# Weight requests on ACT's DMA queue, with four kinds of instructions raised in priority

## Chip, core and metric

The kernel runs on one core of one Trainium2 chip. The metric is device time in microseconds (us) of that core, median over the runs of a measurement; the profile is one further execution of the same program.

## The reference, cut to what matters

One layer of a decoder with two groups of heads is computed for 512 prompt tokens and for 32 new tokens (8 sequences of 4) behind a paged cache of 2048 positions each. All is float32.

```
h = rmsnorm(x, norm_w)                      # x: 544 tokens x 2048
p = h @ w_in                                # w_in: 2048 x 8192
qa, ka, va, za, qb, fb, ib, zb = split(p, 1024 columns each)
o_a = stick_breaking(qa, ka, va)            # 8 heads of 128; new tokens also see the cache
o_b, s = hgrn2(silu(qb), fb, ib, s0)        # 8 heads, gated linear recurrence
m = concat(head_rmsnorm(o_a) * silu(za), head_rmsnorm(o_b) * silu(zb))
y = final_rmsnorm(x + m @ w_out)            # w_out: 2048 x 2048
```

Stick-breaking attention takes A[t,s] = beta[t,s] times the product of (1 - beta[t,j]) over s < j < t with beta = sigmoid(q.k/sqrt(128) + bias), which the kernel computes with exp, ln and a running sum along the keys. Outputs are y, the new keys and values, and the new recurrent states.

## The kernel before, in words

**Stages.** The tokens are loaded, transposed and split into a rounded part and a rest, `h_hi` and `h_lo` (L338 to L356). Then 64 columns of 128 outputs of the input projection follow one another (`group_a`, L927, and `group_b`, L1007, both through `project`, L381), and then the output projection in 8 column groups (L1124 and L1209). Between the matmuls of the projections the TensorE order holds all other work: prompt attention (`attend`, L455), the recurrence (`hgrn`, L705), and attention of the new tokens over the cache (`decode`, L645), which runs from the first heads of group A to about 0.87 of the projections.

**Weights.** Both projections read their weights in 160 pieces of 512 KB (128 of `w_in`, 32 of `w_out`), in the order of `plan` (L239). Each piece goes through three steps. `load_ahead` (L244) requests it from HBM into a `wraw` tile, of which there are three. `split_ahead` (L252) has ACT cast it into `whi` (L259) and DVE subtract that into `wlo` (L260), of which there are two each. `project` multiplies `whi` with `h_hi` and `h_lo`, and `wlo` with `h_hi` (L401). A piece is requested three ahead of the one in use and split one ahead (`weights_piece`, L268). A `wraw` tile is free again when both halves of its split are done; in the output projection also when TensorE has used it for the sample rows (L1115). A `whi` or `wlo` tile is free when TensorE has done its matmuls. When a column is done, DVE takes it out of PSUM with a multiplication (L408).

**Cache.** Pages of keys are requested in units of 1 MB, four DMAs each (`k_fetch`, L534), into three `kpage` tiles; DVE transposes each unit in place (`k_turn`, L550), and TensorE reads it in `dzp` (L678). Pages of values are requested in blocks of 256 KB (`v_fetch`, L556) into ten `vpage` tiles. One step of `decode` uses two key units and eight value blocks.

**Order.** L164 fixes the order of TensorE and of SyncE (SP) to that of the program text, in which `Flow` (L76) places side work between matmuls by estimated costs and delays. SP issues nearly all loads: weights, key pages, value pages, states and queries. It stands at each request until that request's tile is free, and what is behind it waits. The order on ACT, DVE and POOL is made by the scheduler when the kernel is built: of what it reckons ready at a time, it takes the instruction with the lowest number, which counts along the program text. Each engine then runs its list in that order and stands at an instruction that waits. ACT's own DMA queue holds a few small constants at the start (L298 to L307), the rows of x and `fnw` for the end of the kernel (L1161 to L1166), and half of the output rows (L1189, L1207).

Of the kernel before, what the change touches and what calls it, by code (L numbers as in the profile page):

```python
# [9 lines left out]
F32 = mybir.dt.float32  # L10
# [3 lines left out]
ALU = mybir.AluOpType  # L14
# [126 lines left out]
def hybrid_step(ctx: ExitStack, tc: tile.TileContext, x_prompt, x_sample, cache_k, cache_v, state_s, page_table,  # L141
                norm_w, w_in, gain_a, gain_b, sb_bias, lb_logits, w_out, final_norm_w, consts, masks,
                y_prompt, y_sample, k_prompt, v_prompt, s_prompt, k_sample, v_sample, s_sample):
    nc = tc.nc
# [33 lines left out]
    def mm(n):  # L178
        return 4.0 * max(n, 128) / 2.4


    cst = per.tile([P, C_SELH], F32, name="cst")
    ident = cst[:, C_ID:C_ID + P]
# [14 lines left out]
    rbc = per.tile([P, T], F32, name="rbc")  # L198
# [22 lines left out]
    def in_view(kh, col):  # L221
        return w_in_v[:, 8 * kh:8 * kh + 8, col:col + P]

    def out_view(kq, cg):
        return w_out_v[:, 4 * kq:4 * kq + 4, cg * CG:cg * CG + CG]
# [15 lines left out]
    raws = []  # L241
    taken = [0]

    def load_ahead(n):  # L244
        while len(raws) < min(n, len(plan)):
            kind, k, c = plan[len(raws)]
            view = in_view(k, c) if kind == "in" else out_view(k, c)
            raw = wpool.tile([P, 1024], F32, name="wraw", bufs=3)
            nc.sync.dma_start(raw.rearrange("p (k e) -> p k e", k=view.shape[1]), view)
            raws.append(raw)  # L250

    def split_ahead(n):  # L252
        while len(splits) < min(n, len(plan)):
            i = len(splits)
            load_ahead(i + 1)
            pool, kw = (keep[0], {"bufs": 4}) if i >= len(plan) - 4 else (wpool, {})
            hi = pool.tile([P, 1024], F32R, name="whi", **kw)
            lo = pool.tile([P, 1024], F32R, name="wlo", **kw)
            turns.append(nc.scalar.copy(hi, raws[i]))  # L259
            nc.vector.tensor_tensor(lo, raws[i], hi.bitcast(F32), ALU.subtract)  # L260
            k = 8 if plan[i][0] == "in" else 4
            splits.append([t.rearrange("p (k e) -> p k e", k=k) for t in (raws[i], hi, lo)])

    splits = []
    turns = []
    keep = [None]

    def weights_piece(want):  # L268
        i = taken[0]
        assert plan[i] == want  # L270
        taken[0] += 1
        split_ahead(i + 2)
        load_ahead(i + 4)
        return splits[i]
# [11 lines left out]
    for i in range(NB + 1):  # L286
        n = P if i < NB else NS
        xt = xpool.tile([P, D], F32, name=f"xt{i}", bufs=1)
        cuts = (0, D // 4, D // 2, D) if i == 0 else (0, D // 2, D)
        for a, b in zip(cuts, cuts[1:]):  # L290
            nc.sync.dma_start(xt[:n, a:b], xp[i * P:(i + 1) * P, a:b] if i < NB else xs[:, a:b])
            if i == 0 and a == 0:
                nc.sync.dma_start(ident, consts[:, C_ID:C_ID + P])
                nc.sync.dma_start(nw_rows, norm_w[0].rearrange("(h d) -> h d", d=P))
        xts.append(xt)
        if i == 1:
            load_ahead(2)
# [83 lines left out]
    def project(out, col, first=False):  # L381
        ps = [ps_acc.tile([P, 512], F32, name="pacc", tag="acc") for _ in range(2)]
        pieces = [None, None]
        order = [(kh, half, part) for kh in range(2) for part in range(2) for half in range(2)]
        if first:
            order = [(kh, half, part) for half in range(2) for kh in range(2) for part in range(2)]
        for kh, half, part in order:
            if pieces[kh] is None:
                pieces[kh] = weights_piece(("in", kh, col))
            _, hi, lo = pieces[kh]  # L390
            ts = HALVES[half]
            n = ts.stop - ts.start
            if part == 0:
                todo = [(j, hi, x) for j in range(8) for x in (h_hi[kh], h_lo[kh])]
            else:
                todo = [(j, lo, h_hi[kh]) for j in range(8)]
            for s in range(0, len(todo), STEP):
                yield STEP * (n / 2.4 + 2.0)
                for r in range(s, s + STEP):
                    j, a, x = todo[r]  # L400
                    nc.tensor.matmul(ps[half][:, :n], a[:, j, :], x[:, j, ts],  # L401
                                     start=(kh == 0 and part == 0 and r == 0), stop=(kh == 1 and part == 1 and r == 7))
            if kh == 1 and part == 1 and (half or not first):
                if callable(out):
                    out = out()
                for e in range(2) if first else (half,):
                    ts = HALVES[e]
                    nc.vector.tensor_tensor(out[:, ts], ps[e][:, :ts.stop - ts.start], rbc[:, ts], ALU.mult)  # L408


    def gate(hh, zt, sg):
# [122 lines left out]
    def k_fetch(n):  # L534
        while len(kpending) < min(n, len(kunits)):
            t = dp.tile([P, 4, 512], F32, name="kpage", bufs=3)
            b, gp, h2 = kunits[len(kpending)]
            for i in (0, 2, 1, 3):
                src = kpages[page_value(k_held, b, gp, i), :, h2 * 512:h2 * 512 + 512]
                nc.sync.dma_start(t[32 * i:32 * i + 32], src.rearrange("o (s r) e -> (o r) s e", r=32))  # L540
            kpending.append(t)
# [3 lines left out]
    def k_turn(n):  # L545
        while len(turned) < min(n, len(kunits)):
            k_fetch(len(turned) + 1)
            t = kpending[len(turned)]
            flat = t.rearrange("p s e -> p (s e)")
            nc.vector.transpose(flat, flat)  # L550
            turned.append(t.rearrange("p s (g d) -> p g s d", g=4))

    vunits = [(b, gp, hf, i) for b in range(DB) for gp in range(4) for hf in range(2) for i in range(4)]
# [91 lines left out]
    def decode(start, stop):  # L645
# [4 lines left out]
        for step in range(NSTEP):  # L650
# [10 lines left out]
            if keys:  # L661
                k_turn(2 * step + 1)
                yield 0.0, (0.0 if step == 0 else 14000.0), 0.0, 0.0
                k_turn(2 * step + 2)
# [262 lines left out]
    def group_a():  # L927
        nonlocal ap, dp, tp_, later, earlier
        for h in range(H):
            if h == H - 1:  # L930
                k_fetch(3)
            if h == 2:
                for c in (slice(0, 6 * P), slice(6 * P, NM * P)):
                    lvlf = ap.tile([P, 6 * P], F32, name="lt", tag="lvlf", bufs=1)[:, :c.stop - c.start]
                    nc.gpsimd.dma_start(lvlf, masks[:, c])
                    nc.gpsimd.tensor_copy(lvls[:, c], lvlf)
            qts = []

            def qtile():
                qts.append(atile("qt"))  # L940
                return qts[0]

            for i, c in enumerate(project(qtile, h * P, h == 0)):
                if h == 0 and i == 23:
                    flow.wait(lambda: not flow.side)
                    xstack.close()
                    dp = dstack.enter_context(tc.tile_pool(name="dpool", bufs=1))
                    dcon = dp.tile([P, C_TOT - C_LATER], F32, name="dcon")
                    nc.sync.dma_start(dcon, consts[:, C_LATER:])
                    later, earlier = dcon[:, :P], dcon[:, P:]  # L950
                    tp_ = dstack.enter_context(tc.tile_pool(name="tpool", bufs=1))
                    lvls = tp_.tile([P, NM * P], U8, name="lvls")
                    lvl.extend(lvls[:, P * i:P * i + P] for i in range(NM))
                    ap = astack.enter_context(tc.tile_pool(name="apool", bufs=1))
                yield c
            nc.gpsimd.tensor_copy(q_new[:, h, :], qts[0][:, SEQ:])
            nc.gpsimd.dma_start(q_dram[h], qts[0][:, :SEQ])
        flow.add(decode(H / 64, STOP), 2)
        for h in range(H):
            qt = ap.tile([P, SEQ], F32, name="ql", bufs=2)  # L960
            nc.sync.dma_start(qt, q_dram[h])
            kt = atile("kt")
            yield from project(kt, W + h * P)
            vt = atile("vt")
            yield from project(vt, 2 * W + h * P)
            res = {}
            flow.wait(lambda: not a_side or a_side[-1] not in flow.side)
            a_side.append(flow.add(attend(h, qt, kt, vt, res), 0))
            zt = atile("zt")
            yield from project(zt, 3 * W + h * P)  # L970
            sg = ap.tile([P, T], F32, name="sg")
            gate(h, zt, sg)
            res["zt"] = zt
            if "ot" in res:
                a_side.append(flow.add(finish_head(ap, h, res["ot"], zt, 4500.0), 0))
# [293 lines left out]
```

## Time and profile before

| | us |
|---|---|
| median of 3 runs | 1407.9 |
| lowest and highest | 1406.34, 1409.33 |
| the profiled execution, its own time | 1405.46 |
| its span, first to last instruction | 1403.8 |
| TensorE busy in the span | 1331.7 (95%) |
| DVE, ACT, POOL busy | 758.3, 413.6, 311.7 |
| mean granted TensorE clock | 0.985 |

TensorE is called PE in the rows, and its weight loads PEld. A busy share says how long an engine had work, not that the work ran at its peak. Waits are listed by who waited, for whom, in total, how often, and the longest.

### The profile page before, as it was taken

What the parts mean: (1) busy time and instruction counts of PE and PEld (TensorE: products, weight loads), DVE (VectorE), ACT (ScalarE), POOL (GpSimd) and SP (SyncE); (2) the same over time, 40 slices, a digit from 0 to 9 for tenths busy, and PEclk for the clock granted to TensorE, in tenths of its full rate; (3) what the DMA queues carried; (4) which work ended last, traced back from release to release, by engine and by line L of the source; (5) the groups of instructions that cost most, each with busy time, mean ns of one, the idle gap of its engine ahead of it and who ended that gap; (6) DMA issues with size and microseconds to landing.
All of it is one profiled execution on the core that took longest, in us unless ns stands there. A gap on an engine that the chain in (4) does not pass through costs nothing.

```text
span 1403.8 us, 30662 instructions
## 1 busy us (share of the span) xinstructions
PE 1331.7 (95%) x11922; PEld 1215.2 (87%) x11922; DVE 758.3 (54%) x1302; ACT 413.6 (29%) x701; POOL 311.7 (22%) x577
## 2 busy tenths in 40 slices
PE   6999999899999999999989989999999999999997
PEld 6999888798988888888887978889899897988996
DVE  6324555647466474667575674665455658222223
ACT  6211324224233242331222231132323225222223
POOL 3212113112132121132332232121213324111001
PEclk9999999999999999999999999999999999999999
DMA  7338876699989898898888978746523251622223
GB/s 218 109 109 214 200 203 163 174 292 235 280 228 269 236 258 220 229 273 212 247 231 233 274 193 235 229 143 196 149 61 113 65 194 42 240 76 78 89 76 143
DMA packets 245027, 260.69 MB, mean 186 GB/s; under 512 B 13497, under 2 KB 169842, under 8 KB 244178
## 3 DMA queue, kind: packets, MB, share of 16 engines
q1 hardware_dynamic: 237600, 235.00, 60.5%
q0 software_dynamic: 5504, 15.80, 3.3%
q10 hardware_dynamic: 1778, 7.93, 1.5%
q8 instruction: 94, 1.54, 0.5%
q14 instruction: 51, 0.42, 0.1%
HBM read 239.15 MB, written 19.53 MB: 184 GB/s over the span
## 4 chain that ended last, share of the span: by engine, by line
PE 74%; issue 10%; DVE 9%; DMA 3%; ACT 3%; POOL 1%; SPq 0%; DVEq 0%; POOLq 0%; ACTq 0%
PE pacc L401 42%; PE yacc L1106 13%; DVE kpage L550 3%; PE av L688 3%; PE dzp L678 3%; PE sp L746 2%; DMA kpage<-in_cache_k 2%; PE op L507 1%; PE usp L897 1%; PE ysp L1115 1%; DVE wlo L260 1%; DMA wraw<-in_w_in 1%; DVE lt L450 1%; DVE att L803 1%; PE wp L174 1%
## 5 line engine op out<-in xcount | busy, mean ns | idle before, releaser
L401 PE MATMUL pacc<-h_hi,whi 128*128 128x256 f32 (+1 forms) x2048 | 546.4, 299 | 15.2 <-ACT whi L259 9.8
L401 PE MATMUL pacc<-h_lo,whi 128*128 128x256 f32 (+1 forms) x2048 | 530.4, 289 | 0.0
L401 PEld LDWEIGHTS pacc<-h_hi,whi 128*128 128x128 f32 x2048 | 389.1, 190 | 40.1 <-issue 22.9
L401 PEld LDWEIGHTS pacc<-h_lo,whi 128*128 128x128 f32 x2048 | 389.2, 190 | 1.7 <-issue 0.2
L260 DVE TENSOR_TENSOR wlo<-wraw,whi 128x1024 fp32r<-128x1024 f32 x160 | 198.0, 1240 | 199.0 <-PE yacc L1106 78.0
L259 ACT CAST whi<-wraw 128x1024 fp32r<-128x1024 f32 x160 | 166.6, 1046 | 458.3 <-PE pacc L401 312.7
L401 PE MATMUL pacc<-h_hi,wlo 128*128 128x256 f32 (+1 forms) x2048 | 294.6, 292 | 0.0
L401 PEld LDWEIGHTS pacc<-h_hi,wlo 128*128 128x128 f32 x2048 | 269.5, 189 | 13.0 <-issue 12.3
L550 DVE STREAM_TRANSPOSE kpage<-kpage 128x2048 f32<-128x2048 f32 x64 | 146.2, 2296 | 0.2 <-issue 0.2
L1106 PE MATMUL yacc<-whi,m_hi 128*128 128x256 f32 x512 | 130.4, 293 | 0.0
L1106 PE MATMUL yacc<-whi,m_lo 128*128 128x256 f32 x512 | 126.7, 285 | 3.1 <-DVE m_lo L1096 3.0
L1106 PEld LDWEIGHTS yacc<-whi,m_hi 128*128 128x128 f32 x512 | 98.8, 193 | 16.8 <-issue 13.0
L1106 PEld LDWEIGHTS yacc<-whi,m_lo 128*128 128x128 f32 x512 | 99.1, 194 | 3.6 <-DVE m_lo L1096 3.5
L678 PE MATMUL dzp<-kpage,qblk 128*32 128x128 f32 x2048 | 68.3, 281 | 23.1 <-DVE kpage L550 23.0
L678 PEld LDWEIGHTS dzp<-kpage,qblk 128*32 128x32 f32 x2048 | 54.8, 112 | 33.0 <-DVE kpage L550 27.4
L1106 PE MATMUL yacc<-wlo,m_hi 128*128 128x256 f32 x512 | 68.3, 282 | 0.0
L1178 POOL TENSOR_TENSOR y<-y,fnw 128x512 f32<-128x512 f32 (+1 forms) x18 | 26.3, 1477 | 178.7 <-DVE y L1174 111.2
L1106 PEld LDWEIGHTS yacc<-wlo,m_hi 128*128 128x128 f32 x512 | 64.3, 191 | 0.0
L688 PE MATMUL av<-vpage,dwt 128*32 128x512 f32 x512 | 62.2, 600 | 0.0
L658 POOL COPY qblk<-q_new 32x32 f32<-32x32 f32 x128 | 45.7, 357 | 31.0 <-PE dzp L678 25.8
L746 PE MATMUL sp<-bE,kr 128*128 128x192 f32 x256 | 47.4, 326 | 1.9 <-DVE o_s L596 1.4
L803 DVE COPY_PREDICATED att<-lvls,sp 128x192 f32<-128x192 uint8 (+2 forms) x144 | 38.3, 310 | 15.9 <-PE sp L746 14.9
(262 smaller groups left out, 1372.3 us busy)
## 6 DMA issues: line engine op xcount, KB each, us to landing
wraw<-in_w_in SPq DMA_DIRECT2D x128, 512.0 KB, 5.9
kpage<-in_cache_k SPq DMA_DIRECT2D x256, 256.0 KB, 5.5
vpage<-in_cache_v SPq DMA_DIRECT2D x256, 256.0 KB, 5.1
wraw<-in_w_out SPq DMA_DIRECT2D x32, 512.0 KB, 3.5
bst<-in_state_s SPq DMA_DIRECT2D x16, 256.0 KB, 6.2
out<-bst POOLq DMA_DIRECT2D x16, 256.0 KB, 3.9
y<-in_x_prompt ACTq DMA_DIRECT2D x4, 1024.0 KB, 7.4
xt<-in_x_prompt SPq DMA_DIRECT2D x7, 512.0 KB, 5.8
```

The source lines that it names most:

```text
L174: nc.tensor.transpose(out, in_, ident[:k, :k])
L259: turns.append(nc.scalar.copy(hi, raws[i]))
L260: nc.vector.tensor_tensor(lo, raws[i], hi.bitcast(F32), ALU.subtract)
L401: nc.tensor.matmul(ps[half][:, :n], a[:, j, :], x[:, j, ts], start=(kh == 0 and part == 0 and r == 0), stop=(kh == 1 and part == 1 and r = ...
L550: nc.vector.transpose(flat, flat)
L658: nc.gpsimd.tensor_copy(out.rearrange("p h (g x) -> p h g x", g=4)[:, :, :, :DT], q_new[32 * j:32 * j + 32, :, DT * b:DT * b + DT].rearran ...
L678: nc.tensor.matmul(zp[32 * g:32 * g + 32, gp * P:(gp + 1) * P], qb[:, at:at + 32], kt[:, g, :, 32 * j:32 * j + 32], start=(gp == 0 and h2 ...
L688: nc.tensor.matmul(av[hf][32 * i:32 * i + 32, :], wt[:, gp, i, :], vpending[n], start=(gp == 0), stop=(gp == 3))
L746: nc.tensor.matmul(sp[:, i * 192:(i + 1) * 192], kr[:, n * P:(n + 1) * P], moving(n), start=True, stop=True)
L803: nc.vector.copy_predicated(a4[:, :, :, d * hl:], m.unsqueeze(1).to_broadcast([P, 2, u, w]), s4[:, :, :, at:at + w])
L1106: nc.tensor.matmul(out, m[4 * kq + j][:, c], b[:, j, :], start=(kq == 0 and part == 0 and r == 0 and (one or tb % 2 == 0)), stop=(kq == 3 ...
L1178: nc.gpsimd.tensor_tensor(part, part, fnw[:, cs].unsqueeze(1).to_broadcast([P, n, CG]), ALU.mult)
```

## The change

The request of each weight piece moves from SP's queue to ACT's, and four kinds of instructions get a priority number that is lower by 4000: these requests, the two halves of a piece's split, the multiplication that takes a projected column out of PSUM, and the transposition of a key unit. Nothing is computed differently; the TensorE order and the order of what stays on SP are the same.

```
+    URGENT = 4000
...
     def load_ahead(n):
...
-            nc.sync.dma_start(raw.rearrange("p (k e) -> p k e", k=view.shape[1]), view)
+            with tc.high_priority(offset=URGENT):
+                nc.scalar.dma_start(raw.rearrange("p (k e) -> p k e", k=view.shape[1]), view)
...
     def split_ahead(n):
...
-            turns.append(nc.scalar.copy(hi, raws[i]))
-            nc.vector.tensor_tensor(lo, raws[i], hi.bitcast(F32), ALU.subtract)
+            with tc.high_priority(offset=URGENT):
+                turns.append(nc.scalar.copy(hi, raws[i]))
+                nc.vector.tensor_tensor(lo, raws[i], hi.bitcast(F32), ALU.subtract)
...
     def project(out, col, first=False):
...
-                    nc.vector.tensor_tensor(out[:, ts], ps[e][:, :ts.stop - ts.start], rbc[:, ts], ALU.mult)
+                    with tc.high_priority(offset=URGENT):
+                        nc.vector.tensor_tensor(out[:, ts], ps[e][:, :ts.stop - ts.start], rbc[:, ts], ALU.mult)
...
     def k_turn(n):
...
-            nc.vector.transpose(flat, flat)
+            with tc.high_priority(offset=URGENT):
+                nc.vector.transpose(flat, flat)
```

## Rows read from the trace of the kernel before

**Rows 1.** The page's head and busy times: us (share of the span) xinstructions.
```profile
span 1403.8 us, 30662 instructions
...
PE 1331.7 (95%) x11922; PEld 1215.2 (87%) x11922; DVE 758.3 (54%) x1302; ACT 413.6 (29%) x701; POOL 311.7 (22%) x577
```

**Rows 2.** Windows of the start and of decode: busy us (instructions), clock, DMA share, GB/s.
```profile
0.00:35.00 35.00, 24.06 (x149) 21.33 (x150) 23.39 (x43) 23.58 (x41) 13.63 (x18) 0.95 0.78 218
...
105.00:920.00 815.00, 767.59 (x7496) 696.63 (x7498) 491.78 (x786) 237.28 (x401) 181.06 (x381) 0.99 0.85 229
```

**Rows 3.** PE's waits, 105 to 920 us: total us, times, longest.
```profile
PE dzp L678 <- DVE kpage L550: 23.0, 15, 3.4
PE pacc L401 <- ACT whi L259: 8.4, 3, 3.5
PE khp L174 <- DVE att L803: 3.0, 2, 2.7
PE knp L174 <- DVE z L464: 2.8, 2, 1.9
PE pacc L401 <- DVE zt L408: 2.4, 1, 2.4
PE pacc L401 <- DVE kt L408: 1.8, 1, 1.8
PE dwtp L174 <- ACT dz L575: 1.7, 1, 1.7
...
PE detp L174 <- DVE att L758: 1.2, 1, 1.2
```

**Rows 4.** Windows in which the granted clock was low, columns as in rows 2.
```profile
209.00:212.40 3.40, 3.40 (x65) 2.97 (x64) 2.96 (x6) 2.63 (x6) 2.74 (x5) 0.50 0.13 7
270.40:273.90 3.50, 3.22 (x13) 2.69 (x11) 3.00 (x4) 1.56 (x2) 0.00 (x0) 0.51 0.10 28
...
840.50:843.90 3.40, 3.38 (x40) 1.97 (x44) 2.16 (x1) 0.00 (x0) 0.00 (x0) 0.50 0.92 228
```

**Rows 5.** Timeline of ACT, 255 to 275 us: start, us, instruction, [idle before <-releaser].
```profile
266.95 0.63 ACT L447 ACTIVATE lt<-z 128x512 f32<-128x512 f32 x1 [20.90 <-POOL z L465]
...
268.14 1.03 ACT L259 CAST whi<-wraw 128x1024 fp32r<-128x1024 f32 x1
```

**Rows 6.** Timeline of PE, 262 to 275 us.
```profile
269.23 0.39 PE L401 MATMUL pacc<-h_hi,whi 128*128 128x256 f32 x1 [3.47 <-ACT whi L259]
```

**Rows 7.** Timeline of SP's queue, 105 to 270 us.
```profile
237.24 6.36 SPq L540 DMA_DIRECT2D kpage<-in_cache_k  x8
244.43 6.58 SPq L561 DMA_DIRECT2D vpage<-in_cache_v  x8
251.11 4.42 SPq L249 DMA_DIRECT2D wraw<-in_w_in  x3
```

**Rows 8.** Tile wraw, 105 to 920 us: ns min/median/max; us from request to landing.
```profile
L260 DVE TENSOR_TENSOR wlo<-wraw,whi x85: 1170/1215/1928, 108.1 to 905.8; 128x1024 fp32r<-128x1024 f32 x85
L249 SPq DMA_DIRECT2D wraw<-in_w_in x85: 367/400/3155, 116.4 to 907.0; - x85
...
DMA to landing us min/median/max: 4.2/6.9/10.1
```

**Rows 9.** Waits of SP's queue, 105 to 920 us, columns as in rows 3.
```profile
SPq L540 <- PE dzp L678: 199.7, 32, 12.2
SPq L249 <- DVE wlo L260: 58.7, 17, 14.5
```

**Rows 10.** Timeline of DVE, 368 to 392 us.
```profile
385.65 2.07 DVE L450 TENSOR_TENSOR_SCAN lt<-ones_r,lt 128x512 f32<-128x512 f32 x2
...
389.08 2.29 DVE L550 STREAM_TRANSPOSE kpage<-kpage 128x2048 f32<-128x2048 f32 x1
```

**Rows 11.** Timeline of ACT and its queue, 1194 to 1203 us.
```profile
1200.76 1.05 ACT L259 CAST whi<-wraw 128x1024 fp32r<-128x1024 f32 x1 [5.47 <-PE yacc L1106]
1200.77 0.82 ACTq L1161 DMA_DIRECT2D y<-in_x_prompt  x2
```

**Rows 12.** Timeline of the start, 0 to 30 us.
```profile
16.00 0.39 PE L401 MATMUL pacc<-h_hi,whi 128*128 128x256 f32 x1 [1.38 <-ACT whi L259]
```

## The prediction

> **What bounds the kernel now.** I read the page's busy times first, then PE's waits by stage, then the timelines around the longest of them. PE is busy for 1331.7 of 1403.8 us [rows 1], so all its idle time is 72.1 us, and no reordering on other engines can give back more than that, but for the clock. Two thirds of it lie between 105 and 920 us, where decode runs beside the projections: PE is busy for 767.59 of 815 us there, 47.4 idle [rows 2]. It has three kinds. First, PE waits for DVE to transpose a key unit, 23.0 us in 15 waits. Second, it waits for a weight's cast (8.4 us) or for the multiplication that frees a PSUM bank (2.4 and 1.8). Third, it waits for steps of attention and recurrence that DVE or ACT make: 3.0, 2.8, 1.7 and 1.2, together 8.7 [rows 3]. The change raises the instructions behind the first two kinds over those behind the third.
>
> The clock adds to it. In the same stretch there are six windows of 3.4 us in which the granted clock was 0.50, that is 1.2 GHz of 2.4; the first, one more and the last are in [rows 4]. Each comes right after PE stood still: that at 270.4 us follows a wait of 3.47 us for a cast that ended at 269.23 [rows 6]. A window costs 3.4 x (1 - 0.5) = 1.7 us, all six 10.2.
>
> How a cast comes late can be followed. SP issues eight key loads from 237.24, eight value loads from 244.43, and only at 251.11 the weights [rows 7]: each group waits behind the one before, and the key loads wait for a tile that PE frees, 199.7 us in all [rows 9]. ACT meanwhile stands for 20.90 us at an exp of attention, and the cast is behind it in ACT's list; it runs at 268.14 [rows 5], although a weight takes 6.9 us in the median to land [rows 8], so that one requested at 251.11 was there near 258. The list had the cast behind the exp because its weight was to arrive late. That the key transpositions come late has another look: at 389.08 one follows a chain of attention, scans included, that DVE ran without a pause [rows 10].
>
> **The change part by part**, against the profiled execution's own 1405.46 us (span 1403.8 and 1.7 around it). The median of the runs is 1407.9, which is 2.4 above.
>
> *Requests of weights on ACT's queue.* They no longer stand behind key and value loads. Where SP held them back for 7 to 14 us, as by the 6.36 and 6.58 us of the two groups in [rows 7], they can go when the tile is free. With the weight there, the cast takes its place in ACT's list before the exps. The three waits for casts go: bounds 0 and 8.4, and I take 8.4, as the one wait that I followed has just this cause. One of the six windows at half clock goes with them: 1.7.
>
> *Key transpositions first.* 23.0 us lie in 15 of the 64 units. Bounds 0 (the data, not DVE's list, decides) and 23.0. A transposition takes 2.29 us and the longest wait was 3.4 [rows 3, 10], so one that starts a single DVE instruction or two earlier removes a wait whole; yet DVE has pauses in this stretch (491.78 of 815 us busy [rows 2]), and a transposition that was ready could have been put into one. That speaks for data that the scheduler reckons late. I take the middle, 11.5, and half of the window at 840.5 us, which follows such a wait: 0.9.
>
> *The multiplications of L408 first.* Bounds 0 and 4.2; they are ready when PE is done, so the number alone decides. I take 4.0 and one window, 1.7.
>
> *What is pushed back.* Every raised instruction delays one that is not raised by up to its own length, 1.2 us for a split [rows 8] or 2.29 for a transposition. Raised and moved ahead, it also leaves the place where it stood, so the chains behind that place gain. The lower bound is 0. The upper is all 64 transpositions each delaying a chain without slack, 64 x 2.29 = 147 us, far from the 8.7 us that PE waits for such chains now. By the nearest row I take half of that again: 5 lost.
>
> *The issue itself.* 160 requests of 0.4 us each [rows 8] are 64 us on ACT's sequencer. In [rows 11] two DMAs were issued from 1200.77 while the cast from 1200.76 was running, so ACT's own work covers them: 0. Without that cover, 85 x 0.4 = 34 us would lie in a stretch in which ACT is busy for 237.28 of 815.
>
> *A new wait on ACT.* The request of piece i+3 waits until DVE has subtracted piece i, and all of ACT's list stands behind it: the exps of attention, sigmoids of the gates, the copies out of PSUM, and the next casts. SP had 58.7 us of that wait in the stretch [rows 9], where it held up page loads alone. On ACT I take 0, since ACT stands for most of its time already (20.90 us in one wait of [rows 5]); the other end is the slower rival below.
>
> *The start.* The first weights no longer follow the first tokens on SP; three pieces, 1.57 MB, go beside them. Bounds: a gain of the 1.38 us for which the first matmul waited for its cast [rows 12], or a loss of 1.57 MB at 218 GB/s [rows 2], 7.2 us, if tokens come after all of them. I take 1.0 lost, nearer to the first as tokens need not come after all.
>
> *The end.* Rows of x and `fnw` share ACT's queue with the weights near 1200 us. The pieces are three ahead; 0.
>
> The sum: -8.4 - 1.7 - 11.5 - 0.9 - 4.0 - 1.7 + 5 + 1 = -22.2. That gives 1383.3 for the profiled execution and, 2.4 higher, 1385.7 for the median: 1386.
>
> A rule of the Trainium skill speaks against the first term. The trace shows the weights held at SP's sequencer, not in the transfers, which take 6.9 us of which some is contention at a DMA share of 0.85 [rows 2, 8]. The page "DMA: Bandwidth & Descriptors", section "Issuing engines are not separate DMA queues", says that loads started by several engines run on the same 16 DMA engines and interleave, and that starting them on several engines "will only save the time on the sequencer it takes to initiate the DMA". By that rule the queue gives nothing beyond the 0.4 us of an issue, and the sum without the terms of the casts would be -12.1, or 1396. The rows show a sequencer that stands, which the rule leaves out; I keep the term.
>
> **The rivals.**
>
> *Slower: ACT stands at its requests.* At ACT's place in the list the request waits for the subtraction, at the least 1.2 us behind the cast. What stands behind it then reaches DVE late, DVE's results reach PE late, and PE's order is fixed. For it speaks that ACT already has waits of 20.90 us and that PE's waits of the third kind show chains without slack. Against it: ACT is busy for only 29% of the span [rows 1], and the scheduler places a request where it reckons the tile free. The stretch has 85 pieces; if each costs PE more than 22.2 / 85 = 0.26 us, the gain is gone. At 0.55 us each, about half of a subtraction, the loss is 47 us, and the time 1386 + 47 = 1433.
>
> *No difference.* Requests stand behind ACT's long waits as they stood behind SP's; the transpositions keep their places because the data decides; what is left of the gain pays for what is pushed back: 1408, give or take 3. For it: the pauses of DVE. Against it: ACT's waits for attention are few, SP's were in every step.
>
> *All waits of the first two kinds go.* 8.4 + 23.0 + 4.2, three windows of 1.7, nothing pushed back: 40.7, so 1367. Against it speaks the DMA share of 0.85, which leaves little room to bring pages earlier.
>
> **How the numbers follow.** The forecast has 0.45, with its own range 1368 to 1403; the slower rival 0.28, no difference 0.12, all waits gone 0.15. From the forecast and the last come 0.60 for faster by over 0.2% (2.8 us, about what a measurement of this kernel can tell from no change), 0.11 for within it, and 0.29 for slower. A range that leaves out 2 in 10 reaches from 1357 to 1428, the upper end into the middle of the slower rival.
>
> **What would show it.** Right: in the profile of the changed kernel PE's wait for ACT whi between 105 and 920 us is under 1 us, and that for DVE kpage is near 12; fewer than six windows at half clock; weights requested from ACT within a us or two of the subtraction that frees their tile. Wrong: PE waits on khp, knp, dwtp, detp or sp that sum to over 20 us, with ACT's queue waiting for DVE wlo in front of them, shows the slower rival. An unchanged wait of about 23 us for DVE kpage, with landings well before it, shows that priority doesn't move the transpositions. The prediction as a whole is wrong if PE's idle time in decode, now 47.4 us, does not fall.

## The result, and the profile after

The changed kernel takes 1522.6 us in the median of 4 runs (1515.6 to 1527.3), the kernel before beside it 1407.1: a ratio of 1.081, with a 95% interval of 1.0789 to 1.0832. The forecast was 1386 with a range up to 1428, so sign and range were both wrong.

The page's head, busy times and chain shares of the changed kernel:

```profile
span 1525.6 us, 30654 instructions
...
PE 1408.6 (92%) x11922; PEld 1236.6 (81%) x11922; DVE 760.5 (50%) x1302; ACT 419.2 (27%) x702; POOL 306.7 (20%) x577
...
PE 76%; DMA 13%; DVE 4%; issue 4%; ACT 1%; POOL 1%; SPq 0%; ACTq 0%; POOLq 0%; DVEq 0%
PE pacc L405 46%; PE yacc L1112 12%; DMA wraw<-in_w_in 7%; DMA vpage<-in_cache_v 5%; PE av L694 4%; PE sp L752 2%; PE dzp L684 2%; DVE wlo L264 2%; PE op L512 1%; PE ysp L1121 1%; PE usp L903 1%; PE zp L467 1%; DVE kpage L556 1%; DMA xt<-in_x_prompt 1%; PE wp L174 1%
```

The engines do the same work as in [rows 1]; PE alone is "busy" for 77 us more, mostly because a matmul that stands for its page counts as busy (69 us of it are at `av`, 62.2 before and 131.2 after). Two transfers have grown on the chain that sets the end: weights (7%) and value pages (5%). All transfers had 3% of that chain before.

The loss can be placed by two marks that both kernels have: the start of PE's first multiplication with a key page and the end of its last. Before, they lie at 135.0 and 919.2 us, after, at 149.6 and 1039.1. So 14.6 us are lost at the start, 105.2 between the marks (784.2 became 889.4), and 2 behind them. The windows that answer to [rows 2] (decode lies later here), and two with a low granted clock as in [rows 4]:

```profile
0.00:35.00 35.00, 13.77 (x62) 12.36 (x63) 13.44 (x18) 14.93 (x21) 7.96 (x13) 0.76 0.69 217
120.00:1040.00 920.00, 839.57 (x7493) 712.80 (x7496) 488.40 (x783) 242.84 (x403) 178.09 (x381) 0.96 0.76 200
...
318.45:321.90 3.45, 3.14 (x8) 1.48 (x9) 0.00 (x0) 0.00 (x0) 0.00 (x0) 0.51 0.86 266
18.10:35.10 17.00, 7.50 (x34) 7.21 (x35) 8.33 (x12) 10.27 (x17) 6.59 (x5) 0.50 0.44 116
```

In decode the DMA share fell from 0.85 to 0.76: the engines that move data are less loaded, not more. PE's waits there, as in [rows 3], and the one long wait of its weight loads:

```profile
PE av L694 <- DMA vpage<-in_cache_v: 60.7, 42, 5.5
PE dzp L684 <- DVE kpage L556: 6.4, 3, 2.9
PE doff L575 <- DVE dc L455: 5.7, 1, 5.7
PE dwtp L174 <- ACT dz L581: 4.9, 1, 4.9
PE pacc L405 <- DVE bz L413: 1.5, 1, 1.5
```

```profile
PEld av L694 <- DMA vpage<-in_cache_v: 120.3, 78, 6.4
```

The waits that the change was to remove are smaller or gone: 23.0 for kpage became 6.4, the 8.4 for casts nothing. In their place PE waits for value pages, 120.3 us on the weight load (the matmuls' 60.7 lie inside it). Before, that wait was 0.3 us. Less the 8.4, the 16.6 of kpage and the 2.7 that L413 now costs less (4.2 against 1.5), that is 92.6 of the 105.2 us; the clock, 0.96 against 0.99 in [rows 2], has a part in the rest, which I haven't divided further. The granted clock stood at 0.50 for 71.7 us of the window, in 14 stretches.

Why the pages are late is read from SP's queue. Its waits in decode, to be set against [rows 9]:

```profile
SPq L567 <- DMA wraw<-in_w_in: 282.8, 54, 12.5
SPq L545 <- DMA wraw<-in_w_in: 134.6, 20, 9.7
SPq L545 <- PE dzp L684: 55.7, 3, 39.3
```

SP requests no weights any more, and yet it stands 417 us for weights to land. A group of eight value requests that took 6.58 us in [rows 7] takes 22.72 here. This is one of the longest; in the median of all groups of eight it is 14.3 us against 6.5 before:

```profile
295.99 22.72 SPq L567 DMA_DIRECT2D vpage<-in_cache_v  x8
```

The compiled list of SP's instructions says what it waits for. A transfer that has landed raises a counter, its completion semaphore; there are eight for the requests of SP and ACT, DMAHW0 to DMAHW7. Each request waits, besides for its tile, until the earlier transfer that used the same one has landed. The requests of SP and of ACT take the eight in turn, in one common order that the scheduler lays down. These are the eight key requests before that group, and the group (shortened to the semaphore of the turn):

```
kpage  DMAHW4, 5, 6, 7, then 1, 2, then 4, 5      (0 and 3 are missing: ACT's weights have them)
vpage  DMAHW6, 7, 0, 1, 2, 3, 4, 5
```

The third value request waits for DMAHW0 and the sixth for DMAHW3, the two that pieces of weights hold. In the trace just these two come late, at 307.35 and 316.06. The kernel before has the same eight semaphores, but there SP made nearly all requests itself, in the order of the turn, so that the transfer eight requests back had nearly always landed (SP's value requests stood 7.0 us for key pages in decode, its weight requests 3.5 us for weights). The chain of waits from 300 to 330 us shows the price (start, us, what):

```profile
306.14 2.30 DVE kpage L556
308.44 0.34 DVE zt L413
308.79 1.14 DVE wlo L264
309.93 0.02 issue
309.95 6.00 DMA wraw<-in_w_in
315.94 0.02 issue
315.96 0.02 SPq L567
...
316.06 2.66 DMA vpage<-in_cache_v
318.72 0.04 issue
318.76 1.91 PE av L694 x2
```

It is a loop. PE frees a weight's tile by way of cast and subtraction; ACT requests the next piece at once, at 309.95; it lands after 6.00 us; only then may SP request a value page, 2.66 us more; and PE, whose order is fixed, stands for that page and so doesn't come to the matmuls that free the next tile. SP's lead over PE is gone. In this turn an urgent transposition of 2.30 us stands in the loop too.

The start is a second, smaller loss. ACT's list begins (with its queue):

```profile
0.81 3.65 ACTq L252 DMA_DIRECT2D wraw<-in_w_in  x3
...
11.77 1.04 ACT L263 CAST whi<-wraw 128x1024 fp32r<-128x1024 f32 x1 [4.39 <-DMA wraw<-in_w_in]
...
14.58 1.51 ACTq L252 DMA_DIRECT2D wraw<-in_w_in  x2
16.13 3.28 ACTq L302 DMA_DIRECT2D rows<-in_gain_a  x1
...
24.15 2.79 ACT L357 CAST h_hi<-xtmp 128x512 fp32r<-128x512 f32 x5 [10.03 <-DMA rows<-in_lb_logits]
```

The first casts of tokens come at 24.15, behind casts that wait for weights and small constants that wait for their turn among the semaphores. PE stands for 9.35 us meanwhile, and its clock is at the lower level, 0.50, from 18.1 to 35.1:

```profile
26.34 1.11 PE L174 MATMUL xtp<-cst,xt 128*128 128x128 f32 x4 [9.35 <-DVE xtmp L355]
```

### The profile page after: what moved, and what is told of

Read it like the earlier page. It is cut to its first block, busy times and chain, and to the rows that moved or that the text cites. A ratio compares the mean times of both kernels' runs of the same rounds, so it can differ in the third digit from the quotient of the medians.

```text
span 1525.6 us, 30654 instructions
## 1 busy us (share of the span) xinstructions
PE 1408.6 (92%) x11922; PEld 1236.6 (81%) x11922; DVE 760.5 (50%) x1302; ACT 419.2 (27%) x702; POOL 306.7 (20%) x577
## 3 DMA queue, kind: packets, MB, share of 16 engines
q10 hardware_dynamic: 151794, 91.83, 22.2%
q0 software_dynamic: 5504, 15.80, 3.0%
## 4 chain that ended last, share of the span: by engine, by line
PE 76%; DMA 13%; DVE 4%; issue 4%; ACT 1%; POOL 1%; SPq 0%; ACTq 0%; POOLq 0%; DVEq 0%
PE pacc L405 46%; PE yacc L1112 12%; DMA wraw<-in_w_in 7%; DMA vpage<-in_cache_v 5%; PE av L694 4%; PE sp L752 2%; PE dzp L684 2%; DVE wlo L264 2%; PE op L512 1%; PE ysp L1121 1%; PE usp L903 1%; PE zp L467 1%; DVE kpage L556 1%; DMA xt<-in_x_prompt 1%; PE wp L174 1%
## 5 line engine op out<-in xcount | busy, mean ns | idle before, releaser
L405 PE MATMUL pacc<-h_hi,whi 128*128 128x256 f32 (+1 forms) x2048 | 554.1, 302 | 1.5 <-DVE bz L413 1.5
L405 PE MATMUL pacc<-h_lo,whi 128*128 128x256 f32 (+1 forms) x2048 | 537.2, 292 | 1.3 <-DVE h_lo L359 1.3
L405 PEld LDWEIGHTS pacc<-h_hi,whi 128*128 128x128 f32 x2048 | 395.4, 193 | 28.5 <-issue 25.9
L405 PEld LDWEIGHTS pacc<-h_lo,whi 128*128 128x128 f32 x2048 | 395.4, 193 | 3.4 <-DVE h_lo L359 1.5
L694 PE MATMUL av<-vpage,dwt 128*32 128x512 f32 x512 | 131.2, 628 | 60.8 <-DMA vpage<-in_cache_v 60.7
L694 PEld LDWEIGHTS av<-vpage,dwt 128*32 128x32 f32 x512 | 24.4, 113 | 134.6 <-DMA vpage<-in_cache_v 120.3
L684 PE MATMUL dzp<-kpage,qblk 128*32 128x128 f32 x2048 | 65.0, 279 | 6.4 <-DVE kpage L556 6.4
L664 POOL COPY qblk<-q_new 32x32 f32<-32x32 f32 x128 | 41.0, 320 | 55.2 <-PE dzp L684 49.9
```

The source lines that it names most:

```text
L405: nc.tensor.matmul(ps[half][:, :n], a[:, j, :], x[:, j, ts], start=(kh == 0 and part == 0 and r == 0), stop=(kh == 1 and part == 1 and r = ...
L664: nc.gpsimd.tensor_copy(out.rearrange("p h (g x) -> p h g x", g=4)[:, :, :, :DT], q_new[32 * j:32 * j + 32, :, DT * b:DT * b + DT].rearran ...
L684: nc.tensor.matmul(zp[32 * g:32 * g + 32, gp * P:(gp + 1) * P], qb[:, at:at + 32], kt[:, g, :, 32 * j:32 * j + 32], start=(gp == 0 and h2 ...
L694: nc.tensor.matmul(av[hf][32 * i:32 * i + 32, :], wt[:, gp, i, :], vpending[n], start=(gp == 0), stop=(gp == 3))
```

## The experiments

Theory A: the queue does the harm, by the shared semaphores. Theory B: the priorities do it. Theory C: bytes on two queues are in each other's way. The marks are the first and last multiplication with a key page, in us; ratios are to the kernel before, with 95% intervals.

| kernel | weights by | priorities | median us | ratio | marks |
|---|---|---|---|---|---|
| before | SP | no | 1407.1 | 1 | 135.0, 919.2 |
| the change | ACT | yes | 1522.6 | 1.081 [1.0789, 1.0832] | 149.6, 1039.1 |
| e1_prio | SP | yes | 1407.4 | 0.9999 [0.9985, 1.0012] | 133.7, 919.0 |
| e2_queue | ACT | no | 1504.4 | 1.0698 [1.0662, 1.0734] | 142.3, 1016.9 |
| e3_pool | POOL | yes | 1380.4 | 0.9803 [0.978, 0.9826] | 137.4, 891.7 |
| e5_pool_noprio | POOL | no | 1378.0 | 0.9792 [0.9769, 0.9814] | 136.9, 888.2 |

**e1_prio, the priorities alone.**
```
-                nc.scalar.dma_start(raw
+                nc.sync.dma_start(raw
```


> The priorities alone: weights requested by SP as before. Theory A (the queue does the harm: a page's request on SP waits for the landing of a weight that ACT requested late): PE's wait of av for vpage, 120.3 us on the weight load in the changed kernel, falls under 5; first key matmul back near 135 us; time 1385 to 1405. Theory B (the priorities do the harm, by pushing DVE's and ACT's chains back): av waits stay and the time is above 1450.

1407.4 us, 2 above theory A's range: theory B falls, and so does the forecast's own hope for the priorities. PE's waits from 105 to 920 us are nearly those of [rows 3]:

```profile
PE dzp L684 <- DVE kpage L556: 20.7, 15, 3.5
PE pacc L405 <- ACT whi L263: 9.9, 4, 3.5
...
PE pacc L405 <- DVE zt L413: 2.4, 1, 2.4
```

**e2_queue, the queue alone.**
```
-    URGENT = 4000
+    URGENT = 0
```


> The queue alone: weights requested by ACT, no priorities. Theory A: SP still waits for landings of wraw, av for vpage over 60 us, time 1480 to 1540. Theory B: av's wait goes and the time is 1400 to 1415.

1504.4 us, and the weight loads' wait for value pages is 120.2 us in 79 waits, as in the change. The queue alone makes 97 of the 115 us.

**e3_pool, the requests on a queue with semaphores of its own.**
```
-                nc.scalar.dma_start(raw
+                nc.gpsimd.dma_start(raw
```


> Priorities as in the change, weights requested by POOL, whose queue is written by software and has completion semaphores of its own. Theory A: SP no longer waits for wraw; av waits for vpage under 15 us; time 1385 to 1425. Theory C (weights and pages on two queues share the DMA engines, so pages come later whatever SP waits for): pages land later than the 3.7 us of the changed kernel, av's waits stay above 60 us, time 1480 to 1530.

1380.4 us, faster than before and 5 below theory A's range. In the compiled list POOL's transfers have eight other semaphores. PE's waits from 105 to 895 us, then SP's:

```profile
PE dwtp L174 <- ACT dz L581: 5.2, 1, 5.2
PE dzp L684 <- DVE kpage L556: 4.1, 3, 2.9
```

```profile
SPq L545 <- PE dzp L684: 341.5, 31, 77.9
SPq L567 <- DMA kpage<-in_cache_k: 28.0, 42, 1.8
SPq L567 <- PE av L694: 16.1, 1, 16.1
```

SP now waits for PE to free key tiles, which means that it is ahead. The DMA issues of this kernel (KB each, median us to landing), and then of the changed one:

```profile
wraw<-in_w_in POOLq DMA_DIRECT2D x128, 512.0 KB, 6.8
kpage<-in_cache_k SPq DMA_DIRECT2D x256, 256.0 KB, 6.8
vpage<-in_cache_v SPq DMA_DIRECT2D x256, 256.0 KB, 7.4
```

```profile
wraw<-in_w_in ACTq DMA_DIRECT2D x128, 512.0 KB, 5.7
kpage<-in_cache_k SPq DMA_DIRECT2D x256, 256.0 KB, 5.9
vpage<-in_cache_v SPq DMA_DIRECT2D x256, 256.0 KB, 3.7
```

Against theory C: in the fast kernel every transfer takes longer than in the slow one. Value pages land in half the time where PE waits for them; they are late since they are asked for late. POOL's queue also moves the weights in fewer packets (last section); no run parts that from its own semaphores, so what share it has in the 27 us gained on the kernel before is open.

**e4_start, the first five pieces by SP.**
```
+            queue = nc.sync if len(raws) < 5 else nc.scalar
...
-                nc.scalar.dma_start(raw
+                queue.dma_start(raw
```


> As the change, but the first five pieces of weights are requested by SP at their old place; it prices the start. The first key matmul was at 135.0 us before and at 149.6 in the changed kernel. Theory A with the start as a separate loss (ACT's first casts stand behind its own requests): first key matmul at 135 to 138 us, time 1505 to 1512. If the start costs nothing in the end, the time stays at 1520 to 1525.

1512.0 us (1.0727 [1.07, 1.0754]), at the upper end of what was expected, with the first mark at 134.8. The start costs the change 10.6 of its 115 us.

**e5_pool_noprio, POOL's queue without the priorities.**
```
-    URGENT = 4000
+    URGENT = 0
...
-                nc.scalar.dma_start(raw
+                nc.gpsimd.dma_start(raw
```


> POOL's queue alone, without the priorities. Priorities alone gave a ratio of 0.9999, POOL with them 0.9803. If the queue alone makes that gain (weights that land early are cast at their turn by the scheduler's own order): 1378 to 1386. If it takes both, the weight early and the instruction first: 1395 to 1407.

1378.0 us. The queue makes the whole gain. The wait for transposed keys goes without any priority (PE's waits, 105 to 895 us):

```profile
PE pacc L405 <- DVE zt L413: 4.1, 2, 2.4
PE dzp L684 <- DVE kpage L556: 3.8, 2, 2.9
```

**e6_halves, each piece in two requests.**
```
...
-                nc.scalar.dma_start(raw.rearrange("p (k e) -> p k e", k=view.shape[1]), view)
+                nc.scalar.dma_start(dst[:, :m], view[:, :m])
+                nc.scalar.dma_start(dst[:, m:], view[:, m:])
```


> As the change, but each piece of weights is requested in two halves of four rows of blocks: the same bytes, twice as many requests from ACT. Theory A (a page's request waits for the completion of an earlier request that may be one of the weights): twice the weights among the requests, so the waits of av for vpage rise from 120 us to 150 to 200 and the time to 1550 to 1600. Theory C (bytes of two queues in each other's way): the bytes are the same, 1515 to 1535.

1523.1 us (1.0831 [1.0799, 1.0863]): a miss for theory A as I had put it. The weight loads' wait for value pages is 121.5 us, as before the split. I read it so: what counts is not how many requests hold a semaphore but the loop, which runs once per piece however the piece is cut. Theory C was not hurt by this run; e9_eighth was made to part the two.

**e7_mixed, the first 110 pieces by SP, the last 50 by ACT.**
```
+            queue = nc.sync if len(raws) < 110 else nc.scalar
...
-                nc.scalar.dma_start(raw
+                queue.dma_start(raw
```


> As the change, but the first 110 of 160 pieces, all that are requested while pages are fetched, go through SP; ACT requests the last 50. Theory A: no page is requested among ACT's weights, so av's waits are under 5 us and the time is 1403 to 1412, as with the priorities alone. If ACT's requests cost something by themselves (ACT stands at them), the last 50 cost 10 us or more and the time is above 1417.

1409.1 us (1.0023 [1.0004, 1.0041]). Where no pages are fetched, ACT's requests do little harm: 2.9 us more lie behind the last key than in e1_prio (span less the mark: 487.5 against 484.6).

**e8_pool5, five pieces by SP, the rest by POOL, with priorities.**
```
+            queue = nc.sync if len(raws) < 5 else nc.gpsimd
...
-                nc.scalar.dma_start(raw
+                queue.dma_start(raw
```


> As with POOL requesting the weights, but the first five pieces go through SP at their old place, so the first tokens keep their place: PE's 6.3 us of waits for xt go. Expected 1374 to 1380, against 1380.4 with all on POOL; above 1382 if the first tokens did not matter and the late first weights cost something.

1376.3 us (0.9781 [0.9756, 0.9807]); not to be told from e3_pool's 1380.4 by the intervals. The first mark is 135.5, earlier by 1.9.

**e9_eighth, seven eighths by POOL, one eighth by ACT (a quarter of the pieces of the output projection), no priorities.**
```
-    URGENT = 4000
+    URGENT = 0
...
+            m = view.shape[1] - 1
+            nc.gpsimd.dma_start(dst[:, :m], view[:, :m])
+            nc.scalar.dma_start(dst[:, m:], view[:, m:])
```


> Without priorities: POOL requests seven eighths of each piece of weights (three quarters of a piece of w_out), ACT the last block of rows. So ACT's queue carries 1/8 of the bytes of w_in, and its requests stand at the same places as with the whole pieces on ACT. Theory A, in the form left by the halves (a page's request waits for the landing of a piece that PE itself paces, one loop per piece however many requests it has): the loop is back with hardly any bytes on ACT's queue; SP waits for landings of wraw, av waits for vpage 80 to 130 us, time 1480 to 1525, near the 1504.4 of all weights on ACT without priorities. Theory C (bytes or packets of ACT's queue in the way of the pages): with 1/8 of the bytes at most 1/8 of the loss of 97 us, so 1378 to 1392, near the 1378.0 of all on POOL.

1460.7 us (1.0374 [1.0344, 1.0404]). That is 83 of the 126 us that part e5_pool_noprio from e2_queue, with an eighth of the bytes: theory C, which gave at most 14, falls. Theory A has the place right and the size 19 to 64 us too high; the weight loads' wait, put at 80 to 130, is 66.9. SP's waits in decode, the weight loads' wait, and the issues:

```profile
SPq L569 <- DMA wraw<-in_w_in: 244.9, 52, 10.7
SPq L547 <- DMA wraw<-in_w_in: 109.7, 21, 13.2
```

```profile
PEld av L696 <- DMA vpage<-in_cache_v: 66.9, 38, 5.8
```

```profile
vpage<-in_cache_v SPq DMA_DIRECT2D x256, 256.0 KB, 4.2
wraw<-in_w_in POOLq DMA_DIRECT2D x128, 448.0 KB, 5.0
...
wraw<-in_w_in ACTq DMA_DIRECT2D x128, 64.0 KB, 2.7
```

ACT's eighth lands in 2.7 us where a whole piece takes 5.7, so each turn of the loop may be some 3 us shorter. That would fit the smaller loss, but the halves of e6_halves landed in 4.4 us and it lost no less, and no run has varied the landing alone: why an eighth costs less stays open.

**e10_pool5np, as e8_pool5 without priorities.**
```
-    URGENT = 4000
+    URGENT = 0
...
+            queue = nc.sync if len(raws) < 5 else nc.gpsimd
...
-                nc.scalar.dma_start(raw
+                queue.dma_start(raw
```


> The best parts together: first five pieces on SP, the rest on POOL, no priorities. The priorities have moved nothing by more than 3 us where the weights were on SP or POOL, and POOL from the sixth piece gave 1376.3 with them. Expected 1372 to 1377.

1376.7 us (0.9774 [0.975, 0.9798]). By the intervals the versions with POOL can't be told apart; the plainest, e5_pool_noprio, beats both kernels, and all that it needs is one word of the code of before, `sync` to `gpsimd` in the request of a piece.

**e11_vpool, weights on ACT, value pages on POOL, no priorities.**
```
-    URGENT = 4000
+    URGENT = 0
...
-            nc.sync.dma_start(t, vpages[at, ...
+            nc.gpsimd.dma_start(t, vpages[at, ...
```
The edit also has POOL read the page numbers of these requests, and orders each request behind the fourth before it.

> Weights on ACT's queue without priorities (1504.4 us), but the value pages are requested by POOL, whose requests have completion semaphores of their own; key pages stay on SP. Theory A: a value page can no longer wait for a piece of weights, the loop is cut where PE waits, av's waits for vpage (120.2 us on the weight load) fall under 20 and the time to 1380 to 1430; SP's key requests still wait over 100 us for landings of wraw, which PE hardly feels (3.8 us of waits for kpage). Theory C or any other harm done by weights on ACT's queue as such: av's waits stay above 60 us, 1480 or more.

1453.3 us (1.0327 [1.0309, 1.0344]). The wait of av for value pages is gone, as theory A has it, though the weights are on ACT's queue as in e2_queue; no harm of that queue to pages shows but by the semaphores. The number was missed by 23 us, for I took the keys to be safe. With SP left to key requests, these stand for the weights instead, and PE feels it (PE's waits over the whole span, then SP's):

```profile
PE dzp L689 <- DVE kpage L556: 44.3, 24, 6.0
```

```profile
SPq L545 <- DMA wraw<-in_w_in: 448.6, 54, 19.2
```

The wait for keys was 3.8 us in e5_pool_noprio, so it is 40 of the 75 us between the two. The rest isn't divided; POOL has more to do here.

## Why the prediction was wrong, point by point

**Requests of weights on ACT's queue: the step that failed.** "They no longer stand behind key and value loads" is true: in the change each of the pieces 16 to 98 (counted from 0) was requested 0.03 us after its tile was free, against 5.9 us in the mean before (start of the request less the end of the subtraction that freed the tile). The casts went with it, -8.4, as written. What the step left out is the way back: with two engines issuing, a key or value load on SP stands until a weight that ACT requested has landed. The sum has no term for that wait; SP stood 417 us so, and PE's weight loads 120.3 us behind it, against the -22.2 of the sum. PE's idle time in decode, which had to fall, rose from 47.4 to 80.4 us (in the longer window), and the stretches at half clock, of which there were to be fewer than six, are 14. The profile of before could not show the size of that wait, but it hints at the resource: SP's value requests there wait 7.0 us, 11 times, for key pages that SP itself had requested earlier. I asked what queues behind the request on ACT, and not who waits for the piece to land.

**Key transpositions first: -11.5 by priority was wrong.** With priorities alone 20.7 of 23.0 us stay (e1_prio), with POOL's queue alone 3.8 (e5_pool_noprio). So the lower bound was right for the priorities. What decided was the time at which pages are asked for, since SP no longer stood at weights between them, and that was worth more than the term.

**L408 first: -4.0** was 0: 2.4 and 1.8 us stay in e1_prio.

**What is pushed back, +5** (half of 8.7 would be 4.4), can't be told from what the priorities gain: on SP's and POOL's queue the two together are 0 (e1_prio against before, e3_pool against e5_pool_noprio: within 3 us). On ACT's queue the priorities cost 18 us (1522.6 against 1504.4): 7.3 at the first mark, most of the rest between the marks (889.4 against 874.6 us in the profiled executions). Why there is not shown: transpositions have 1.5% of the chain between the marks in both.

**The issue on ACT, 0,** stands within 3 us for the last 50 pieces (e7_mixed); in decode no run shows it apart from the loop.

**The new wait on ACT, 0,** and with it the slower rival: steps of attention and recurrence cost PE 11.8 us in all (5.7, 4.9, and two of 0.7 and 0.5), and of those that it named only dwtp's 4.9, below the 20 set for it. The rival had the sign, not the place.

**The start, +1.0,** was mis-sized and outside its bounds: 10.6 by e4_start. I priced the bytes; the trace shows the loss in ACT's order, where casts that wait for weights and constants stand before the first casts of tokens (without the priorities the same bytes put the first mark 7.3 us earlier).

**The size of the gain** was nearly right for a queue that doesn't tie SP, 1378.0 with e5_pool_noprio against 1386, but partly by luck: that isn't the change that was forecast, and the sum had the keys' 11.5 us from the priorities. The rule of the Trainium skill that was weighed there ("DMA: Bandwidth & Descriptors", "Issuing engines are not separate DMA queues") says that starting transfers on several engines saves only the time that a sequencer takes to initiate them. The prediction put it at 1396, the priorities' terms included; the priorities gave nothing (e1_prio), and the queue alone gave 29 us. What the rule leaves out is the standing: SP had stood 58.7 us for weights' tiles [rows 9] with pages behind it. In e3_pool it stands 341.5 us for key tiles, 199.7 before, so it runs further ahead. How much of the 29 us is the saved standing, and how much the saved initiating (85 requests of 0.4 us, 34 us of SP's time in decode), no run parts.

Not tried: weights on ACT with semaphores that pages don't share, or with pages earlier in the scheduler's order. That the sharing is the cause of the loss rests on SP's waits in the trace, the compiled list, and e3_pool, e9_eighth and e11_vpool together.

## What to carry to other kernels

Before moving requests to another queue, list the completion semaphores that each request waits for: if two queues draw on one set in turn, a prefetch on the first stands for the transfers of the second, and a transfer that the compute engine paces takes the prefetch's lead away. Look at which transfer the issuing engine waits for, not only at how long a transfer takes; pages that land fast and are waited for are asked for late. And test each part of a change alone: here one part did nothing, and the other did all, in either direction by the engine that it was given.

## What the runs showed of the hardware

A request costs POOL 900 ns in the median where it costs ACT 374 (512 KB pieces of `w_in`), and POOL's busy time rose from 311.7 to 443.1 us with it in e3_pool; PE's waits for POOL stayed at 2.9 us. The same 160 pieces are 150,016 packets on ACT's queue (151,794 less the 1,778 of before) and 23,040 on POOL's in e3_pool (28,544 less the 5,504 of before).
